# Feed-forward input products by seven quarter products: sums of weight quarters by accumulating transfers, gated tiles split at the output product

## The chip, the cores and the metric

The kernel runs on one core of one Trainium2 chip. The core has TensorE (matrix products, called PE in the profile, with its weight loads as PEld), VectorE (DVE), ScalarE (ACT), GpSimd (POOL) and SyncE (SP, which here only issues transfers). The engines run side by side and wait for one another through semaphores; transfers between the chip's memory and the core's on-chip memory run on 16 DMA engines. The metric is the device time of one execution in microseconds (us); lower is better.

## The reference

Two layers of a trunk over 512 tokens of width 1024, all in float32. Each layer is, in this order: half of a gated feed-forward, a mixer (a state-space scan and an attention side by side), half of a second gated feed-forward, and a gated per-layer input. What matters here is the feed-forward, which occurs four times:

```
def swiglu_ffn(x, w_in, w_out):
    g, u = jnp.split(x @ w_in, 2, axis=-1)
    return (jax.nn.silu(g) * u) @ w_out

h = x + 0.5 * swiglu_ffn(rms_norm(h, ffn1_norm[i]), ffn1_w_in[i], ffn1_w_out[i])
```

`w_in` is 1024 x 5632 (2816 columns for `g`, 2816 for `u`), `w_out` is 2816 x 1024. The input product `x @ w_in` is a 512 x 1024 by 1024 x 5632 product.

## The kernel before, in words

**Layout.** Activations are kept transposed: features lie in the 128 partitions, the 512 tokens along the free axis. A feature tile is 128 x 512; there are 8 of them for the trunk `h` and 22 (`KF`) for the hidden layer.

**Precision.** Each float32 operand is split into two parts of a faster type, `hi` (a rounded copy, made by ACT) and `lo` (the rest, made by DVE). A product of a weight block and a feature tile is then three matmuls: `hi` by `hi`, `hi` by `lo`, `lo` by `hi` (`acc_wx`, L344 to L346).

**Weights.** `plan_layer` lists every weight unit in the order in which the products take them. A unit is up to 128 x 1024 numbers, 512 KB. `load_one` issues its transfer on SP into one of `NRAW` = 4 buffers called `raw` (L226); `split_one` makes `hi` (L240, ACT) and `lo` (L241, DVE) in one of `NW` = 3 pairs of buffers. `weights(key)`, called before each product, keeps the transfers `LOOK_DMA` = 5 units and the splits `LOOK_SPLIT` = 2 units ahead.

**The order of the work.** The Python code fixes which instruction works on what and the order of priority. The order in which each engine executes them is made when the program is built, from a model of the execution: an instruction whose inputs and buffers are there can be put ahead of earlier ones. 74 buffers of 128 x 512 (`slots`) and 8 banks for results (`banks`) are handed out in the order in which they came free, which also limits how far ahead an instruction can go.

**The feed-forward** (`ffn`). The norm of the input (`Norm`) puts its gain into the operands as each tile of `h` is finished (`add_operand`, L382 and L383) and adds up the squares; the factor per token, `norm.rb`, is applied later. For each of the 22 tiles `f` there is one product for `g` and one for `u`, 24 matmuls of 512 columns each. `evac` then takes the pair out of its banks: DVE multiplies `g` by the factor per token (L465), ACT applies SiLU (L467), DVE multiplies by `u` (L468), and the result is split at once into `hi` and `lo` (`halves`, L357 and L358), which stay for the output product. The output product makes 8 tiles, each over all 22 hidden tiles in three weight units; DVE scales (L500), adds to `h` (L502), and the next norm's operand and square follow.

**Around it.** Before the first feed-forward, `x` comes in by 8 transfers (L274) and is transposed on TensorE (L1252). Before the second one the mixer's last output products finish tiles of `h`. After the second comes the per-layer input (`ple`), whose two loads (`ple_load`, L1146) are issued before that feed-forward. In the mixer, POOL does some products and sums (L773, L804), and attention keeps its probabilities in slots (`pr` in `scores`).

Of the kernel before, what the change touches and what calls it, by code (L numbers as in the profile page):

```python
# [17 lines left out]
P = 128  # L18
# [21 lines left out]
NSLOT = 74  # L40
NRAW = 4
NW = 3
LOOK_DMA = 5
LOOK_SPLIT = 2

# 2*pi as a sum of pieces; the first two have 12 bits, so that 11 bits times them are exact
# [20 lines left out]
class _Slots:  # L67
    """Buffers of one size, each with a tag of its own, handed out in the order they came free."""
# [17 lines left out]
def kernel(ctx: ExitStack, tc: tile.TileContext, a: dict, out: bass.AP):  # L86
# [20 lines left out]

    def sm(tag, shape, dt=F32, bufs=None):
        uid[0] += 1
        return small.tile(list(shape), dt, tag=tag, name=f"{tag}_{uid[0]}", bufs=bufs)  # L110
# [8 lines left out]
    units = []  # L119

    def unit(key, nk, cols, *loads):
        units.append((key, nk, cols, loads))
# [4 lines left out]
    def plan_ffn(i, nm, w_in, w_out):  # L127
        for f in range(KF):
            unit((i, nm, "g", f), KD, P, (None, kview(w_in, 0, KD, f * P, P)))
            unit((i, nm, "u", f), KD, P, (None, kview(w_in, 0, KD, FF + f * P, P)))  # L130
# [74 lines left out]
    loaded, split = [], []  # L205
    later = deque()

    def load_one():
        for _ in range(4 if len(loaded) > 2 else 0):
            if later:  # L210
                later.popleft()()
        key, nk, cols, loads = units[len(loaded)]
        raw = p_raw.tile([P, 1024], F32, tag="raw", name=f"raw{len(loaded)}")
        v = raw[:, :nk * cols].rearrange("p (k f) -> p k f", k=nk)
        for where, src in loads:
# [10 lines left out]
            nc.sync.dma_start(out=dst, in_=src)  # L226
        loaded.append((raw, nk, cols))
# [4 lines left out]
    def split_one():  # L232
        j = len(split)
        while len(loaded) <= j:
            load_one()
        raw, nk, cols = loaded[j]
# [3 lines left out]
        A.copy(hi[:, :n], raw[:, :n])  # L240
        V.tensor_tensor(lo[:, :n], raw[:, :n], hi[:, :n].bitcast(F32), op=ALU.subtract)  # L241
        loaded[j] = None
# [3 lines left out]
    taken = [0]  # L246

    def weights(key):
# [3 lines left out]
        while len(loaded) < min(j + 1 + LOOK_DMA, len(units)):  # L252
            load_one()
# [53 lines left out]
    tri = const.tile([P, P], F32, name="tri")        # 1 where row <= column  # L307
    stri = const.tile([P, P], F32, name="stri")      # 1 where row > column
# [6 lines left out]
    mk_l = const.tile([P, P], BF16, name="mk_l")     # row 0: queries of the first chunk  # L315
    mk_r = const.tile([P, P], BF16, name="mk_r")     # row 0: keys of the second chunk
# [44 lines left out]
    class Norm:  # L361
        """RMS norm over the feature tiles added to it: the gain goes into the products'
        operand, the per-token factor is applied to what the products give."""
# [26 lines left out]
        def add_part(self, y, src, cs):  # L390
            """Some columns of the last tile."""
# [6 lines left out]
        def add_square(self, src):  # L398
            if self.acc is None:
                self.acc = S()  # L400
                A.activation(self.acc.ap, src, AF.Square)
            else:
                sq = S()
                A.activation(sq.ap, src, AF.Square)
                V.tensor_tensor(self.acc.ap, self.acc.ap, sq.ap, op=ALU.add)
                slots.put(sq)
# [45 lines left out]

    def gain(i, nm):
        return lambda k: vcol(i, nm, k)
# [4 lines left out]
    def ffn(i, nm, norm, nxt, start=lambda: None, tables=lambda: None):  # L459
        hid = []  # L460

        def evac(bg, bu):
            # the per-token factor of `u` is applied after the output product
            g = S()
            V.tensor_tensor(g.ap, bg.ap, norm.rb.ap, op=ALU.mult)  # L465
            banks.put(bg)
            A.activation(g.ap, g.ap, AF.Silu)  # L467
            V.tensor_tensor(g.ap, bu.ap, g.ap, op=ALU.mult)  # L468
            banks.put(bu)
            hi, lo = S(F32R), S(F32R)  # L470
            halves(g.ap, hi.ap, lo.ap)
            slots.put(g)
            hid.append((hi, lo))

        X = norm.ops
        held = []
        for f in range(KF):
            bg, bu = B(), B()
            acc_wx(bg.ap, weights((i, nm, "g", f)), X)
            if f == 0:  # L480
                start()
                norm.stats()
            if f == 2:
                norm.spread()
            acc_wx(bu.ap, weights((i, nm, "u", f)), X)
            held.append((bg, bu))
            if f >= 2:
                for pair in held:
                    evac(*pair)
                held = []  # L490
            if f == 4:
                tables()
        norm.drop(rb=False)
        H = [(p.ap, q.ap) for p, q in hid]
        for m in range(KD):
            b = B()
            for k0 in range(0, KF, 8):
                acc_wx(b.ap, weights((i, nm, "o", m, k0)), H, k0, k0 == 0, k0 + 8 >= KF)
            t = S()
            V.scalar_tensor_tensor(out=t.ap, in0=b.ap, scalar=0.5, in1=norm.rb.ap, op0=ALU.mult, op1=ALU.mult)  # L500
            banks.put(b)
            V.tensor_tensor(h[m].ap, h[m].ap, t.ap, op=ALU.add)  # L502
            slots.put(t)
            nxt.add(h[m].ap)
        slots.put(norm.rb)
        for p, q in hid:
            slots.put(p, q)

# [4 lines left out]
    def rope_tables():  # L513
# [23 lines left out]
        # the turns were counted from a rounded quotient: one may be left  # L537
# [16 lines left out]
    def rotate(src, cosv, sinv, n):  # L554
        """src: [P, n, 64] rows to rotate; cosv and sinv of that shape. A buffer [P, n, 64]."""
# [10 lines left out]
    def merge(dense, sparse, every):  # L566
        """Issue `sparse`'s steps in between `dense`'s, one for each `every` us of the latter."""
# [12 lines left out]
    def mixer(i, norm, nxt):  # L580
# [11 lines left out]
        # dt and the rotary key  # L592
# [7 lines left out]
        def conv_a(j, b):  # L600
            """Evacuate tile j of xBC and convolve it."""
# [14 lines left out]
        # decays and steps, with tokens in the partitions  # L616
# [46 lines left out]
        # cumulated log decays: from the chunk's start, to its end, and the whole  # L663
# [12 lines left out]
        # rotary key, doubled for the two halves of the queries  # L676
# [215 lines left out]
        # latents of queries and keys  # L892
# [91 lines left out]
        def scores(hd, qb):  # L984
# [15 lines left out]
            pr = S()  # L1000
# [8 lines left out]
        # where the blocks of the transposed probabilities lie: buffer and first column  # L1009
# [3 lines left out]
        def flip(hd, qb, pr, pt):  # L1013
# [4 lines left out]
            slots.put(pr)  # L1018
# [294 lines left out]
```

## Time and profile before

| what | value |
|---|---|
| median of 3 runs | 2345.74 us (2345.72 to 2346.37) |
| span of the profiled execution, first to last instruction | 2343.0 us; no other time of it is given, and the runs' median is 2.7 us above it |
| TensorE busy | 2330.0 us, 99% of the span |
| VectorE, ScalarE, GpSimd busy | 1245.1, 885.3, 126.0 us |
| transfers | 209.73 MB, 90 GB/s in the mean; SP's queue takes 30.6% of the 16 engines' time |
| granted TensorE clock | 0.999 of full speed |

The profile is of one execution. "Busy" for TensorE counts from the start of a matmul to its modelled end, and since matmuls are pipelined these lengths overlap; what one costs in a stream is read from the distance between starts. Lines such as L344 are lines of the kernel before, and a line can be that of a helper which many places call. In the lists of groups a row has the line, the engine, the operation, output and input with their shapes, the count, the busy time in us and the mean length in ns, and behind the last bar the idle time before these instructions with what ended it.

### The profile page before, as it was taken

The numbers are of one execution on the slowest core, as the hardware profiler recorded it, in microseconds if no ns is written. First come the engines' busy times: TensorE is split into PE (matmuls) and PEld (weight loads), VectorE is DVE, ScalarE is ACT, GpSimd is POOL, SyncE is SP. The second block draws the span as 40 slices with busy tenths as digits, with TensorE's granted clock in tenths as the row PEclk, the third lists the DMA queues.
The fourth block names the chain that finished last, engine by engine and source line by source line (L and its number), as shares of the span: only waits on it lengthen the run. The fifth ranks groups of instructions, "written<-read, shape, count | busy, mean of one in ns | idle before, by whom it ended". The sixth has DMA issues, their size and how long they took to land.

```text
span 2343.0 us, 27624 instructions
## 1 busy us (share of the span) xinstructions
PE 2330.0 (99%) x10950; PEld 1933.4 (83%) x10950; DVE 1245.1 (53%) x1944; ACT 885.3 (38%) x1388; POOL 126.0 (5%) x136
## 2 busy tenths in 40 slices
PE   9999999999999999999999999999999999999998
PEld 7888888888888888888888888888888888888887
DVE  5543345688676434434644443466876764443345
ACT  4322224455455322222432222244544543222224
POOL 0000000223000000000000000011320000000000
PEclk9999999999999999999999999999999999999999
DMA  5333333221222333332333333332112223333322
GB/s 159 97 99 98 91 96 102 88 61 43 75 81 72 100 99 99 92 95 88 100 103 99 92 95 99 95 101 82 49 53 64 93 74 106 96 94 95 99 75 84
DMA packets 396110, 209.73 MB, mean 90 GB/s; under 512 B 19438, under 2 KB 390348, under 8 KB 395980
## 3 DMA queue, kind: packets, MB, share of 16 engines
q1 hardware_dynamic: 395980, 207.96, 30.6%
q8 instruction: 86, 1.41, 0.3%
q14 instruction: 44, 0.36, 0.0%
HBM read 205.83 MB, written 2.10 MB: 89 GB/s over the span
## 4 chain that ended last, share of the span: by engine, by line
PE 99%; DMA 0%; SPq 0%; DVE 0%; ACT 0%; POOL 0%; issue 0%
PE b L344 28%; PE b L345 28%; PE b L346 28%; PE b L353 2%; PE b L352 2%; PE b L354 2%; PE b L852 1%; PE b L1017 1%; PE b L1043 0%; PE b L833 0%; PE b L836 0%; PE b L993 0%; PE b L990 0%; PE b L1044 0%; PE b L992 0%; PE b L991 0%
## 5 line engine op out<-in xcount | busy, mean ns | idle before, releaser
L344 PE MATMUL b<-s,hi 128*128 128x512 f32 (+2 forms) x2906 | 1139.1, 393 | 0.0
L346 PE MATMUL b<-s,lo 128*128 128x512 f32 (+2 forms) x2906 | 1131.2, 390 | 0.0
L345 PE MATMUL b<-s,hi 128*128 128x512 f32 (+2 forms) x2906 | 1130.9, 390 | 0.0
L240 ACT CAST hi<-raw 128x1024 fp32r<-128x1024 f32 (+3 forms) x428 | 412.1, 963 | 1121.7 <-PE b L345 656.2
L241 DVE TENSOR_TENSOR lo<-raw,hi 128x1024 fp32r<-128x1024 f32 (+3 forms) x428 | 480.6, 1124 | 349.7 <-ACT hi L240 338.7
L346 PEld LDWEIGHTS b<-s,lo 128*128 128x128 f32 (+1 forms) x2906 | 545.4, 188 | 113.4
L344 PEld LDWEIGHTS b<-s,hi 128*128 128x128 f32 (+1 forms) x2906 | 545.8, 188 | 112.6 <-issue 2.4
L345 PEld LDWEIGHTS b<-s,hi 128*128 128x128 f32 (+1 forms) x2906 | 545.7, 188 | 112.5 <-issue 2.9
L468 DVE TENSOR_TENSOR s<-b,s 128x512 f32<-128x512 f32 x88 | 60.5, 691 | 254.6 <-PE b L346 250.9
L465 DVE TENSOR_TENSOR s<-b,s 128x512 f32<-128x512 f32 x88 | 60.1, 690 | 202.3 <-PE b L346 202.3
L430 POOL TENSOR_TENSOR nr<-nv,half 128x4 f32<-128x4 f32 (+1 forms) x14 | 19.1, 1366 | 1759.9 <-DVE nv L422 1759.1
L357 ACT CAST s<-b 128x128 fp32r<-128x128 f32 (+2 forms) x196 | 66.8, 360 | 102.6 <-DVE s L358 34.0
L358 DVE TENSOR_TENSOR s<-b,s 128x128 fp32r<-128x128 f32 (+2 forms) x196 | 75.4, 402 | 33.2 <-ACT s L357 31.7
L352 PE MATMUL b<-hi,s 128*128 128x512 f32 (+1 forms) x208 | 77.9, 375 | 0.0
L353 PE MATMUL b<-hi,s 128*128 128x512 f32 (+1 forms) x208 | 77.2, 371 | 0.0
L354 PE MATMUL b<-lo,s 128*128 128x512 f32 (+1 forms) x208 | 76.2, 366 | 0.0
L358 DVE TENSOR_TENSOR s<-s,s 128x512 fp32r<-128x512 f32 x104 | 71.0, 685 | 1.1 <-ACT s L357 0.7
L357 ACT CAST s<-s 128x512 fp32r<-128x512 f32 x104 | 64.6, 622 | 5.6 <-DVE s L976 4.6
L382 ACT ACTIVATE s<-s,vec 128x512 fp32r<-128x512 f32 x56 | 40.4, 722 | 56.4 <-DVE s L502 46.7
L608 DVE SCALAR_TENSOR_TENSOR s<-s,vec,s 128x511 f32<-128x511 f32 (+2 forms) x72 | 60.8, 848 | 0.6
L500 DVE SCALAR_TENSOR_TENSOR s<-b,s 128x512 f32<-128x512 f32 x32 | 22.1, 692 | 65.4 <-PE b L346 65.4
L467 ACT ACTIVATE s<-s 128x512 f32<-128x512 f32 x88 | 54.8, 626 | 0.4
(221 smaller groups left out, 1612.9 us busy)
## 6 DMA issues: line engine op xcount, KB each, us to landing
raw<-in_ffn_w_in_dram SPq DMA_DIRECT2D x176, 512.0 KB
raw<-in_ffn_w_out_dram SPq DMA_DIRECT2D x64, 512.0 KB
raw<-in_w_in_mix_dram SPq DMA_DIRECT2D x50, 512.0 KB
raw<-in_w_out_mix_dram SPq DMA_DIRECT2D x32, 512.0 KB
raw<-in_ffn_w_out_dram SPq DMA_DIRECT2D x32, 384.0 KB
raw<-in_w_ple_gate_dram SPq DMA_DIRECT2D x16, 512.0 KB
raw<-in_w_q_b_dram SPq DMA_DIRECT2D x16, 192.0 KB
s<-in_x_dram SPq DMA_DIRECT2D x8, 256.0 KB
```

Of the source, the lines that this page charges most:

```text
L240: A.copy(hi[:, :n], raw[:, :n])
L241: V.tensor_tensor(lo[:, :n], raw[:, :n], hi[:, :n].bitcast(F32), op=ALU.subtract)
L344: mm(b, lhsT=hi[:, kk, cs], rhs=xh, start=st, stop=False)
L345: mm(b, lhsT=hi[:, kk, cs], rhs=xl, start=False, stop=False)
L346: mm(b, lhsT=lo[:, kk, cs], rhs=xh, start=False, stop=en)
L352: mm(b, lhsT=xh[:, cs], rhs=hi[:, kk], start=first, stop=False)
L353: mm(b, lhsT=xl[:, cs], rhs=hi[:, kk], start=False, stop=False)
L354: mm(b, lhsT=xh[:, cs], rhs=lo[:, kk], start=False, stop=last)
L357: A.copy(hi, src)
L358: V.tensor_tensor(lo, src, hi.bitcast(F32), op=ALU.subtract)
L468: V.tensor_tensor(g.ap, bu.ap, g.ap, op=ALU.mult)
L608: V.scalar_tensor_tensor(out=y[:, s:], in0=x[:, :T - s], scalar=wc(3 - s), in1=y[:, s:], op0=ALU.mult, op1=ALU.add)
```

## The change

The input product is done by blocks of 2 x 2 quarters: tokens in two halves of 256 (`HT`), the 8 feature tiles in even and odd ones (paired as `e`, `o`), and weight columns in two halves of 256 within groups of 512. There are 11 groups for each feed-forward: five for `g` and five for `u` of four hidden tiles each (`GROUPS`), and a last one, `"m"`, with two tiles of `g` and two of `u`. For a group seven products of quarters (Strassen's scheme in the form with 15 additions) take the place of eight.

- **Operands.** `NormQ` takes the place of `Norm` ahead of a feed-forward. Per pair of feature tiles it makes four half-width sums or differences (three on DVE, one on POOL) and splits the seven half-width operands, which occupy 28 slots until the last group has used them.
- **Weight quarters.** Products 1, 2 and 3 take a quarter as it is loaded (by SP, 512 KB each, with rows of 256 columns). Products 5, 6, 4 and 7 take sums: 5 is the buffer of 1 with another quarter added, 6 that of 5 with one more, 4 that of 6, and 7 that of 3. The addition is a transfer issued by POOL that adds what it loads to what the buffer holds (`accum_op=ADD`), issued when the buffer's previous content has been split.
- **Order.** In step `n` the products are 1 of group n, 7 of n-1, 5 of n, 4 of n-1, 3, 6 and 2 of n (`ORDER`). A product is 24 matmuls of 256 columns, into a bank of two tiles by 256 tokens. Products are accumulated onto one another in the bank where they can be; in between, ACT copies a bank aside (`copied`) and DVE adds or subtracts (`combined`).
- **Gating.** `finish` applies the factor per token and SiLU to a `g` group and keeps the result, and multiplies it by the `u` group when that is done. The tiles stay in float32 (22 slots) and are split into `hi` and `lo` ahead of the first output tile, by halves of the tokens.
- **Buffers.** 71 slots for 74; 6 `raw` buffers for 4; transfers are kept 3 loads ahead of the split. Temporaries of the output product and of the sums of squares, and attention's probabilities, come from the `raw` buffers (`tmp`). The loads of the per-layer input go behind the last output tile (`between`).

The core of the diff:

```diff
+ORDER = ((1, 0), (7, 1), (5, 0), (4, 1), (3, 0), (6, 0), (2, 0))
+GROUPS = [(x, q) for q in range(KF // 4) for x in "gu"] + [("m", KF // 4)]
...
+            first = {1: (0, 0), 2: (1, 0), 3: (1, 1)}
+            after = {5: (1, 0, 1), 6: (5, 1, 1), 4: (6, 1, 0), 7: (3, 0, 1)}
...
+        if j in more:
+            held[more[j]] = x
+            _, nk, cols, _, (_, loads) = units[more[j]]
+            place_in(x, nk, cols, loads,
+                     lambda dst, src: G.dma_start(out=dst, in_=src, accum_op=ALU.add))
...
+        def quarters(self, e, o):
+            a11, a21, a12, a22 = e[:, :HT], e[:, HT:], o[:, :HT], o[:, HT:]
+            s, t = S(), S()
+            s1, s2, s3, s4 = s[:, :HT], s[:, HT:], t[:, :HT], t[:, HT:]
+            V.tensor_tensor(s1, a21, a22, op=ALU.subtract)
+            V.tensor_tensor(s2, s1, a11, op=ALU.subtract)
+            G.tensor_tensor(s3, a11, a21, op=ALU.subtract)
+            V.tensor_tensor(s4, a12, s2, op=ALU.add)
+            for p, x in ((1, a11), (2, a12), (5, s1), (6, s2), (4, a22), (7, s3), (3, s4)):
+                y = S(F32R)
+                halves(x, y[:, :HT], y[:, HT:])
+                self.O[p].append(y)
...
+        def product(bank, n, p, first):
+            hi, lo = weights((i, nm, n, p))
+            ops = norm.O[p]
+            for f in range(2):
+                o = bank[:, f * HT:(f + 1) * HT]
+                cs = slice(f * P, (f + 1) * P)
+                for k in range(4):
+                    x = ops[k]
+                    more = dict(skip_group_check=not first)
+                    mm(o, lhsT=hi[:, k, cs], rhs=x[:, :HT], start=first and f == k == 0, stop=False, **more)
+                    mm(o, lhsT=hi[:, k, cs], rhs=x[:, HT:], start=False, stop=False, **more)
+                    mm(o, lhsT=lo[:, k, cs], rhs=x[:, :HT], start=False, stop=f == 1 and k == 3, **more)
...
+                if m == 0:
+                    for f in range(k0, k0 + nk):
+                        hi, lo = S(F32R), S(F32R)
+                        for a in range(2):
+                            ts = slice(a * HT, (a + 1) * HT)
+                            halves(hid[a][f // 2][:, (f % 2) * HT:(f % 2 + 1) * HT], hi[:, ts], lo[:, ts])
+                            if f % 2:
+                                slots.put(hid[a][f // 2])
```

More of the change, by code (lines that the diff above doesn't have):

```diff
@@ L106, with tmp @@
     uid = [0]
+    def tmp():
+        uid[0] += 1
+        return p_raw.tile([P, 1024], F32, tag="raw", name=f"tmp{uid[0]}")[:, :T]
     def sm(tag, shape, dt=F32, bufs=None):
@@ L116, with raw @@
     G = nc.gpsimd
+    raws = []
     units = []
+    def raw(nk, cols, *loads):
+        raws.append((nk, cols, loads))
+        return len(raws) - 1
     def unit(key, nk, cols, *loads):
-        units.append((key, nk, cols, loads))
+        units.append((key, nk, cols, raw(nk, cols, *loads), None))
     def kview(w, k0, nk, c0, n):
@@ L203, with place_in @@
         plan_layer(i)
-    loaded, split = [], []
+    loaded, split, held = [], [], {}
     later = deque()
[L208 to L214, printed above, removed]
+    more = {u[4][0]: j for j, u in enumerate(units) if u[4] is not None}
+    def place_in(t, nk, cols, loads, start):
+        v = t[:, :nk * cols].rearrange("p (k f) -> p k f", k=nk)
         for where, src in loads:
@@ L225, in load_one @@
                     dst = v[:, k, h * 64:(h + 1) * 64]
-            nc.sync.dma_start(out=dst, in_=src)
-        loaded.append((raw, nk, cols))
+            start(dst, src)
+    def load_one():
+        for _ in range(4 if len(loaded) > 2 else 0):
+            if later:
+                later.popleft()()
+        t = p_raw.tile([P, 1024], F32, tag="raw", name=f"raw{len(loaded)}")
+        place_in(t, *raws[len(loaded)], lambda dst, src: nc.sync.dma_start(out=dst, in_=src))
+        loaded.append(t)
     def small_load(out, in_):
@@ L233, in split_one @@
         j = len(split)
-        while len(loaded) <= j:
-            load_one()
-        raw, nk, cols = loaded[j]
+        _, nk, cols, r, _ = units[j]
+        if r is not None:
+            while len(loaded) <= r:
+                load_one()
+            held[j] = loaded[r]
+        x = held.pop(j)
         n = nk * cols
@@ L451, with __init__, add_operand, drop_product @@
         rb = None
+    class NormQ(Norm):
+        def __init__(self, *args):
+            super().__init__(*args)
+            self.O = {p: [] for p in range(1, 8)}
+            self.pair = []
+        def add_operand(self, src, operand=True):
+            w = self.gain(self.k)
+            self.k += 1
+            x = S()
+            A.activation(x.ap, src, AF.Copy, scale=w)
+            self.pair.append(x)
+            if len(self.pair) == 2:
+                e, o = self.pair
+                self.pair = []
+                self.quarters(e, o)
+                slots.put(e, o)
+        def quarters(self, e, o):
[10 more added lines that the diff above has]
+                self.O[p].append(y)
+            slots.put(s, t)
+        def drop_product(self, p):
+            slots.put(*self.O.pop(p))
     def gain(i, nm):
```

183 lines of the change are left out of this document (124 added, 59 removed).

## The prediction

> **What bounds the kernel now.** I read the page's busy shares first, then its chain, then TensorE in order of time where its matmuls narrow, then the other engines by stretches.
>
> ```profile
> span 2343.0 us, 27624 instructions
> PE 2330.0 (99%) x10950; PEld 1933.4 (83%) x10950; DVE 1245.1 (53%) x1944; ACT 885.3 (38%) x1388; POOL 126.0 (5%) x136
> PE 99%; DMA 0%; SPq 0%; DVE 0%; ACT 0%; POOL 0%; issue 0%
> ```
>
> The chain is TensorE for 99% of the span, so a matmul saved is time saved as long as nothing else becomes late. The profile's "busy" is a pipelined length, so I price a matmul by the distance between starts. Near the end the kernel itself goes from 512 to 256 moving columns (TensorE in order of time; start, length, line):
>
> ```profile
> 2290.49 0.39 PE L344 MATMUL b<-s,hi 128*128 128x512 f32 x1
> ...
> 2323.15 0.39 PE L344 MATMUL b<-s,hi 128*128 128x512 f32 x1
> ...
> 2323.83 0.28 PE L344 MATMUL b<-s,hi 128*128 128x256 f32 x1
> ...
> 2329.22 0.28 PE L344 MATMUL b<-s,hi 128*128 128x256 f32 x1
> ```
>
> 144 matmuls lie between the first two starts: 32.66/144 = 0.2268 us. 45 lie between the last two: 5.39/45 = 0.1198 us. Half the columns cost 53% rather than 50%: 107.0 ns for 256 columns plus 12.8 ns fixed. Each matmul also has its weight load; 187 to 192 ns long, so I looked at whether loads hold up the narrow ones:
>
> ```profile
> 2324.06 0.19 PEld L344 LDWEIGHTS b<-s,hi 128*128 128x128 f32 x1
> 2324.18 0.19 PEld L345 LDWEIGHTS b<-s,hi 128*128 128x128 f32 x1
> ```
>
> They start 0.12 apart and overlap; the load does not set 0.188 as the pace.
>
> **The change, part by part.** *Matmuls.* Before, four feed-forwards make 44 tiles each from 8 weight blocks with 3 matmuls: 4 x 44 x 8 x 3 = 4224 of 512 columns, 958.0 us. After, 4 x 11 groups x 7 products x 24 = 7392 of 256 columns, 885.6 us. Saved: 72.4 us. One eighth of 958 would be 120; the fixed 12.8 ns on 3168 more instructions and their share takes the rest.
>
> The Trainium skill (TensorE: Matmul & The Clock Gate, "Back-to-back issue gap") gives N/2.4 + 2.5 ns between warm matmuls, so about 109 and 216 ns; an estimate from it would be a saving of 104 us. The trace has a fixed part of 12.8 ns, not 2.5, and decides.
>
> *Evacuations in the input stage.* Rows for the pieces (groups by line with shapes kept apart):
>
> ```profile
> L240 ACT CAST hi<-raw 128x1024 fp32r<-128x1024 f32 x342 | 359.2, 1051 | 946.9 <-PE b L345 538.5 <-issue 383.8 <-PE b L353 22.8
> L241 DVE TENSOR_TENSOR lo<-raw,hi 128x1024 fp32r<-128x1024 f32 x342 | 422.2, 1235 | 322.3 <-ACT hi L240 311.5
> L465 DVE TENSOR_TENSOR s<-b,s 128x512 f32<-128x512 f32 x88 | 60.1, 690 | 202.3 <-PE b L346 202.3
> L467 ACT ACTIVATE s<-s 128x512 f32<-128x512 f32 x88 | 54.8, 626 | 0.4
> L1245 ACT COPY s<-b 128x512 f32<-128x512 f32 x4 | 2.3, 579 | 0.0
> L358 DVE TENSOR_TENSOR s<-b,s 128x256 fp32r<-128x256 f32 x16 | 6.7, 419 | 1.6 <-ACT s L357 1.6
> L383 DVE SCALAR_TENSOR_TENSOR s<-s,vec,s 128x512 fp32r<-128x512 f32 x56 | 41.9, 749 | 24.1 <-ACT s L382 24.1
> ```
>
> A group lasts 168 x 0.1198 = 20.1 us on TensorE. DVE then has 7 weight splits (8.6), 3 combinations and 4 finishes (7 x 0.69 = 4.8): 13.4 us. ACT has 7 casts (7.4), 3 copies (1.7) and, in a gate group, 4 SiLU (2.5): 11.6 us. Both lie under TensorE; a bank's copy or combination has one product of another bank (2.87 us) as cover, where it needs under 0.7 (uncovered only in the first and last group). Cost 0.
>
> *Operands at a feed-forward's start.* Instead of one 0.749 us DVE step per tile (6.0 us for 8) there are, per pair, three half-width sums and seven half-width splits on DVE (one more sum is POOL's): 4 x 10 x 0.42 = 16.8, so 10.8 us more, and ACT gets 28 half-width casts for 8 full ones. Where that lands (busy time by stretches; columns: stretch, its length, then busy us of PE, PEld, DVE, ACT, POOL, granted clock, DMA share, GB/s):
>
> ```profile
> 6.00:21.00 15.00, 13.11 (x54) 10.65 (x53) 13.78 (x19) 12.45 (x21) 0.00 (x0) 1.00 1.01 254
> 747.00:765.00 18.00, 18.00 (x81) 14.90 (x80) 17.52 (x25) 13.10 (x20) 0.00 (x0) 1.00 0.39 114
> 1170.00:1180.00 10.00, 10.00 (x46) 8.29 (x45) 5.94 (x8) 3.78 (x5) 0.00 (x0) 1.00 0.53 157
> 255.00:275.00 20.00, 20.00 (x90) 16.57 (x89) 7.43 (x9) 5.65 (x7) 0.00 (x0) 1.00 0.32 94
> ```
>
> At the kernel's start (first row) and before a second feed-forward (second row; it comes twice) DVE is full, so the last operand comes 10.8 us later. TensorE can take the other three pairs of the first three products meanwhile, 54 x 0.1198 = 6.5 us. Exposed: 4.3 to 10.8; I take 6 three times. Before layer 1's first feed-forward (third row) DVE is 59% busy: 0 to 4, I take 2. Together 20 us (13 to 36). Next late there is nothing: the groups behind have slack.
>
> *Gated tiles split at the output product.* 44 half-width splits, 18.5 us of DVE, leave the loop and stand before the first output tile, which is 66 x 0.2268 = 15.0 us long. The fourth row shows DVE with 7.43 of 20 us already used there: if all splits ran there, 7.4 + 18.5 - 20 = 6 us would show, 24 for four. But the written order isn't the executed one; work with its inputs ready is drawn forward:
>
> ```profile
> 27.21 0.17 DVE L653 TENSOR_SCALAR d_a<-d_a 128x16 f32<-128x16 f32 x1 [6.07 <-ACT d_a L641]
> ```
>
> This line belongs to the mixer, whose stage follows the whole first feed-forward. The splits can start as buffers come free (each product of the last group frees four), so most fit into DVE's free third of the last group. I take 1 us each, 4 in all (0 to 24).
>
> *Weight traffic.* SP's 176 input loads become 132, and 176 accumulating transfers go to POOL's queue, where nothing else waits in this stage. Each waits until its buffer's previous content is split. Tightest link, quarter 1 to quarter 5: a split starts two products ahead and takes 2.3 us:
>
> ```profile
> 120.26 1.06 ACT L240 CAST hi<-raw 128x1024 fp32r<-128x1024 f32 x1 [3.84 <-PE b L345]
> 121.35 1.23 DVE L241 TENSOR_TENSOR lo<-raw,hi 128x1024 fp32r<-128x1024 f32 x1 [0.21 <-ACT hi L240]
> ```
>
> (120.26 to 122.58). Product 5 comes two products after product 1, so the transfer has 4 x 2.87 - 2 x 2.3 = 6.9 us before TensorE waits. If it is late, ACT's cast of that quarter waits, behind it on ACT the next cast and bank copies, and TensorE waits for those. No accumulating transfer stands in this trace. Nearest rows, plain loads at the start and elsewhere:
>
> ```profile
> 1.25 2.05 SPq L274 DMA_DIRECT2D s<-in_x_dram  x4
> 4.20 2.04 PE L1252 MATMUL b<-ident,s 128*128 128x128 f32 x8 [1.59 <-DMA s<-in_x_dram]
> 2.00:10.00 8.00, 4.25 (x17) 3.04 (x17) 3.88 (x8) 4.69 (x6) 0.64 (x4) 1.00 1.02 271
> 680.00:690.00 10.00, 10.00 (x54) 8.14 (x53) 6.73 (x21) 3.96 (x12) 0.00 (x0) 1.00 0.46 155
> L430 POOL TENSOR_TENSOR nr<-nv,half 128x4 f32<-128x4 f32 x12 | 17.7, 1477 | 1711.7 <-DVE nv L422 1711.0 <-DVE nv L427 0.7
> ```
>
> 256 KB land 2.9 us after issue; the other 256 KB at 271 GB/s add 1.0: 3.9 us for a plain quarter, the lower end (a plain copy's work is contained in it, so no gain below). Upper end: source, destination and sum each moved like a plain copy, 3.9 + 2 x 1.9, plus 1.5 for POOL as in its L430: 9.2. The middle is 6.6, just inside 6.9: I take 0, and up to (9.2 - 6.9) x 44 = 101 us. Volume: rows of 1 KB go at 155/0.46 = 337 GB/s of full engines, so a group's three plain loads need 4.7 us and four accumulations 6.2 at plain price, 18.7 at three times it: 10.9 to 23.4 us against 20.1, so 0 to 3.3 x 44 = 145 us.
>
> The Trainium skill speaks against cheap sums: Collectives: The Full Stack ("The bandwidth ceiling: the fold count and why AG ≠ RS ≠ AR") says an add in the transfer engines halves the rate because it reads two sources through one ring. An estimate by it is 4.7 + 12.5 = 17.2 of 20.1 us, which still fits. No run so far shows it.
>
> *Small moves.* The two loads of the per-layer input go behind the output product; the gate's first product (24 x 0.2268 = 5.4 us) covers their 2.9, else some 3 us twice. Temporaries and attention probabilities share the six load buffers: 0, at worst 10 us.
>
> **Sum.** 2343.0 - 72.4 + 20 + 4 = 2294.6 against the profiled span; the median of the runs is 2.7 us above that span, so about 2297.
>
> **Rivals.**
> 1. *Accumulations late (other side).* From 6.9 us on each group loses the excess. The gain of 48 is eaten at 48/44 = 1.1 us, at 8.0 us per transfer; at 9.2 the time is 2398, and by volume at three times the plain price 2442. For it: the bounds include it, nothing in the trace measures it, and 86% of the engines' time would go at a price of two copies. Against: the engines are at 0.32 of their time now (fourth row of the stretches), and the later links (5 to 6, 3 to 7) have 2.9 us more each.
> 2. *Everything hidden.* If TensorE finds enough ready work at the starts and before the output, 24 falls to 0: 2273. For it: TensorE is busy 18.00 of 18.00 in the second row, with DVE full there as well. Against: DVE's 10.8 us are real, and the 6.5 us of cover are less.
> 3. *Nothing drawn forward.* 36 at the starts, 24 at the outputs, 10 of buffers: 2343.0 - 72.4 + 70 + 2.7 = 2343, no change.
> 4. *The narrow pace doesn't last.* At one load per 0.188 us, 7392 would cost 1390 us: 2800. The 45 starts exclude it but for a per cent.
>
> **How the numbers follow.** Forecast 0.45 (2283 to 2325), hidden 0.16, nothing drawn forward 0.10, late accumulations 0.28, the pace 0.01. A measurement of this kernel tells 0.2% (5 us). Faster: 0.45 + 0.16 and half of rival 3: 0.66. Same: 0.05. Slower: 0.29. The range leaves out under a tenth below and some of the dearer half of rival 1: 2268 to 2425; the faster cases' own is 2268 to 2330.
>
> **What would show it.** Input matmuls of 256 columns at 0.12 us starts and about 20 us per group; TensorE idle mostly within 15 us of a feed-forward's start, released by DVE splits of operands; no idle at the output's start. Rival 1: ACT's weight casts released by DMA, once per group, and TensorE gaps at every fifth product. I am wrong if TensorE has gaps inside the groups, or if its starts in the new products lie further apart than 0.122.

## The result, and the profile after

The changed kernel takes 2496.06 us (median of 4 runs, 2493.02 to 2501.34) against 2345.73 us before: 1.0643 times as long, with a 95% interval of 1.0628 to 1.0658. The forecast was 2297, and its range ended at 2425. The profiled execution of the changed kernel took 2493.02 us, 1.8 us more than its span.

The page of the changed kernel: span, engines, the two transfer queues, the chain.

```profile
span 2491.2 us, 35639 instructions
PE 2334.5 (94%) x14118; PEld 2071.8 (83%) x14118; DVE 1512.1 (61%) x2440; ACT 1120.2 (45%) x1860; POOL 381.1 (15%) x344
...
q1 hardware_dynamic: 288972, 184.89, 25.4%
q0 software_dynamic: 101376, 92.29, 24.9%
...
PE 64%; DMA 19%; DVE 6%; issue 6%; ACT 4%; POOL 1%; SPq 1%; ACTq 0%; POOLq 0%; DVEq 0%
```

The chain that was TensorE for 99% now goes through transfers for 19% and through DVE, ACT and "issue" for another 16%. The queue rows give the price of an addition. Plain loads (q1) moved 184.89 MB in 25.4% of the engines' span, which is 292 GB/s of full engines; adding transfers (q0) moved 92.29 MB in 24.9%, which is 149 GB/s: half.

Where the time goes is read from TensorE's waits and from what ACT waits for (engine, line, what it waited for: us in all, times, longest).

```profile
PE b L567 <- ACT hi L286: 87.9, 50, 4.6
PE b L569 <- DVE lo L287: 18.0, 18, 4.5
PE b L568 <- DVE s L413: 14.9, 8, 4.0
...
PE b L401 <- DVE lo L287: 5.4, 4, 1.5
```

```profile
ACT hi L286 <- DMA raw<-in_ffn_w_in_dram: 291.9, 67, 8.2
```

L286 is ACT's cast of a weight quarter, L567 the first matmul that uses it. So the sign that the prediction gave for rival 1 is there: casts released by transfers, and TensorE released by casts. It is inside the groups, as TensorE in order of time shows for the steady part of the first feed-forward (all its waits of over half a microsecond between 60 and 215 us; start, length, line, and in brackets the idle time before):

```profile
63.21 0.39 PE L567 MATMUL b<-s,hi 128*128 128x256 f32 x1 [2.92 <-ACT hi L286]
88.61 0.58 PE L567 MATMUL b<-s,hi 128*128 128x256 f32 x1 [3.24 <-ACT hi L286]
111.55 0.39 PE L567 MATMUL b<-s,hi 128*128 128x256 f32 x1 [1.12 <-ACT hi L286]
135.17 0.39 PE L567 MATMUL b<-s,hi 128*128 128x256 f32 x1 [2.96 <-ACT hi L286]
158.31 0.39 PE L567 MATMUL b<-s,hi 128*128 128x256 f32 x1 [0.99 <-ACT hi L286]
184.01 0.58 PE L567 MATMUL b<-s,hi 128*128 128x256 f32 x1 [4.65 <-ACT hi L286]
207.33 0.39 PE L567 MATMUL b<-s,hi 128*128 128x256 f32 x1 [1.41 <-ACT hi L286]
```

One gap per group, 22.9 to 25.7 us apart, where a group was forecast at 20.1. It is always at the same place of a group. The casts of weights come in the order 1, 7, 5, 4, 3, 6, 2, and a transfer is issued after the casts of 1, 5, 3 and 6 but not after 7, 4 and 2; that pattern tells which cast is which. Around the gap at 184.01, on ACT and on POOL:

```profile
161.91 1.05 ACT L286 CAST hi<-raw 128x1024 fp32r<-128x1024 f32 x1 [1.12 <-PE b L568]
...
171.24 2.00 ACT L286 CAST hi<-raw 128x1024 fp32r<-128x1024 f32 x2 [5.16 <-DMA raw<-in_ffn_w_in_dram]
...
173.62 1.05 ACT L286 CAST hi<-raw 128x1024 fp32r<-128x1024 f32 x1
182.92 1.05 ACT L286 CAST hi<-raw 128x1024 fp32r<-128x1024 f32 x1 [8.24 <-DMA raw<-in_ffn_w_in_dram]
183.87 0.58 ACT L596 COPY s<-b 128x512 f32<-128x512 f32 x1
```

```profile
164.50 1.28 POOL L295 DMA_DIRECT2D raw<-in_ffn_w_in_dram  x1 [3.26 <-DVE lo L287]
173.84 1.28 POOL L295 DMA_DIRECT2D raw<-in_ffn_w_in_dram  x1 [8.05 <-DVE lo L287]
177.43 1.28 POOL L295 DMA_DIRECT2D raw<-in_ffn_w_in_dram  x1 [2.31 <-DVE lo L287]
```

The cast at 161.91 is product 1's. Its quarter's transfer for product 5 starts on POOL at 164.50, and the cast of 5 can go at 171.24: 6.7 us. ACT had waited 5.2 us for it; TensorE, which begins product 5 at 173.06, felt 0.3 us of that (before its matmul at 173.60, below). Then the transfer for 6 starts at 173.84, with the one for 7 beside it from 177.43, and 6's cast goes at 182.92: 9.1 us. TensorE's gap ends 1.09 us later. Every gap in the fence above follows a cast of product 6. Five of the seven casts had waited for their transfer (2.6 to 8.2 us). The two before the smallest gaps, at 111.55 and 158.31, ACT shows as released by TensorE; but they too went 5.9 us after POOL's transfer for 6 (104.52 to 110.45 and 151.36 to 157.22), which is about as long as a landing takes (6.2 us in the median, see e2).

TensorE's and VectorE's rows show one thing more:

```profile
173.60 0.39 PE L569 MATMUL b<-s,lo 128*128 128x256 f32 x1
...
185.09 0.41 PE L569 MATMUL b<-s,lo 128*128 128x256 f32 x1
...
188.60 0.40 PE L569 MATMUL b<-s,lo 128*128 128x256 f32 x2
```

```profile
175.92 1.22 DVE L287 TENSOR_TENSOR lo<-raw,hi 128x1024 fp32r<-128x1024 f32 x1
183.99 1.23 DVE L287 TENSOR_TENSOR lo<-raw,hi 128x1024 fp32r<-128x1024 f32 x1 [6.86 <-ACT hi L286]
```

TensorE's order, made when the program was built, is not quite `ORDER`: the first two matmuls of product 6 (184.01 and 184.39) stand ahead of all of product 3. The matmul at 185.09 already uses a `lo`, while VectorE ends the `lo` of 6 only at 185.22 (183.99 + 1.23), so it belongs to 3; the rest of 6 follows from 188.60, where two L569 stand side by side. The weights of product 3 were split by 177.14, but it is accumulated onto the bank of product 5, and ACT's copy of that bank stands behind the cast of 6 (183.87). So the late cast of 6 held up the 2.87 us of product 3 as well. No run changes this order alone.

A gap costs more than its idle time (stretch, length, then busy us of PE, PEld, DVE, ACT, POOL, granted clock, DMA share, GB/s):

```profile
179.00:184.00 5.00, 0.37 (x4) 0.16 (x2) 0.01 (x1) 1.08 (x2) 0.00 (x0) 0.99 1.16 192
184.00:187.50 3.50, 3.49 (x16) 3.49 (x17) 2.95 (x3) 1.39 (x2) 1.28 (x1) 0.52 0.02 3
187.50:194.00 6.50, 6.50 (x56) 6.50 (x55) 2.70 (x3) 2.58 (x3) 1.28 (x1) 1.00 0.81 169
```

While two adding transfers run, the engines are full (first row). After the gap TensorE gets half its clock for 3.4 us (second row: 0.52, and 16 matmuls where the last row's pace would make 30). The Trainium skill (TensorE: Matmul & The Clock Gate, "Part 1: The HAM clock gate") has the clock halved after an idle window of some 3.4 us, until some 3.4 us of work have passed. The trace agrees where the gap was 4.65 us and the half clock 3.4; after the shorter gap of 2.92 us at 63.21 the clock was 0.50 from 64.5 to 67.9 as well.

### The profile page after: what moved, and what is told of

Its sections match the earlier page's. It is cut to its first block, busy times and chain, and to the rows that moved or that the text cites. A ratio compares the mean times of both kernels' runs of the same rounds, so it can differ in the third digit from the quotient of the medians.

```text
span 2491.2 us, 35639 instructions
## 1 busy us (share of the span) xinstructions
PE 2334.5 (94%) x14118; PEld 2071.8 (83%) x14118; DVE 1512.1 (61%) x2440; ACT 1120.2 (45%) x1860; POOL 381.1 (15%) x344
## 3 DMA queue, kind: packets, MB, share of 16 engines
q1 hardware_dynamic: 288972, 184.89, 25.4%
q0 software_dynamic: 101376, 92.29, 24.9%
## 4 chain that ended last, share of the span: by engine, by line
PE 64%; DMA 19%; DVE 6%; issue 6%; ACT 4%; POOL 1%; SPq 1%; ACTq 0%; POOLq 0%; DVEq 0%
DMA raw<-in_ffn_w_in_dram 19%; PE b L399 13%; PE b L401 13%; PE b L400 13%; PE b L567 5%; PE b L568 4%; PE b L569 4%; ACT hi L286 3%; DVE lo L287 3%; PE b L407 1%; PE b L408 1%; PE b L409 1%; PE b L1017 1%; DVE s L413 1%; PE b L1182 1%
## 5 line engine op out<-in xcount | busy, mean ns | idle before, releaser
L287 DVE TENSOR_TENSOR lo<-raw,hi 128x1024 fp32r<-128x1024 f32 (+3 forms) x560 | 642.1, 1149 | 685.5 <-ACT hi L286 684.4
L286 ACT CAST hi<-raw 128x1024 fp32r<-128x1024 f32 (+3 forms) x560 | 547.7, 981 | 968.9 <-PE b L400 372.9
L567 PE MATMUL b<-s,hi 128*128 128x256 f32 x2464 | 726.0, 295 | 102.3 <-ACT hi L286 87.9
L568 PE MATMUL b<-s,hi 128*128 128x256 f32 x2464 | 715.8, 291 | 14.9 <-DVE s L413 14.9
L569 PE MATMUL b<-s,lo 128*128 128x256 f32 x2464 | 709.5, 291 | 18.1 <-DVE lo L287 18.0
L567 PEld LDWEIGHTS b<-s,hi 128*128 128x128 f32 x2464 | 489.6, 199 | 123.4 <-ACT hi L286 100.1
L399 PE MATMUL b<-s,hi 128*128 128x512 f32 (+1 forms) x1498 | 590.6, 396 | 0.0
L401 PE MATMUL b<-s,lo 128*128 128x512 f32 (+1 forms) x1498 | 584.0, 391 | 5.4 <-DVE lo L287 5.4
L400 PE MATMUL b<-s,hi 128*128 128x512 f32 (+1 forms) x1498 | 582.2, 389 | 0.0
L569 PEld LDWEIGHTS b<-s,lo 128*128 128x128 f32 x2464 | 486.4, 199 | 22.9 <-DVE lo L287 22.6
L568 PEld LDWEIGHTS b<-s,hi 128*128 128x128 f32 x2464 | 489.9, 199 | 17.8 <-DVE s L413 17.5
L295 POOL DMA_DIRECT2D raw<-in_ffn_w_in_dram x192 | 247.6, 1335 | 803.4 <-DVE lo L287 757.5
L401 PEld LDWEIGHTS b<-s,lo 128*128 128x128 f32 x1498 | 280.7, 187 | 66.2 <-DVE lo L287 7.7
L400 PEld LDWEIGHTS b<-s,hi 128*128 128x128 f32 x1498 | 281.1, 188 | 58.1 <-issue 2.9
L399 PEld LDWEIGHTS b<-s,hi 128*128 128x128 f32 x1498 | 281.2, 188 | 56.7 <-issue 2.4
L413 DVE TENSOR_TENSOR s<-s,s 128x256 fp32r<-128x256 f32 (+1 forms) x304 | 118.9, 433 | 4.3 <-ACT s L412 3.9
L596 ACT COPY s<-b 128x512 f32<-128x512 f32 x132 | 76.5, 579 | 8.7 <-PE b L569 8.7
```

Of the source, the lines that this page charges most:

```text
L286: A.copy(hi[:, :n], x[:, :n])
L287: V.tensor_tensor(lo[:, :n], x[:, :n], hi[:, :n].bitcast(F32), op=ALU.subtract)
L295: lambda dst, src: G.dma_start(out=dst, in_=src, accum_op=ALU.add))
L399: mm(b, lhsT=hi[:, kk, cs], rhs=xh, start=st, stop=False)
L400: mm(b, lhsT=hi[:, kk, cs], rhs=xl, start=False, stop=False)
L401: mm(b, lhsT=lo[:, kk, cs], rhs=xh, start=False, stop=en)
```

## The experiments

Two theories stood at first: that the adding transfers are late (their price), and that something which comes with them is (issue by POOL, the waits, 69 MB more). Later two readings of the price had to be told apart: full engines, or single landings on links that are too short. All kernels are variants of the changed one; "link" is the number of products, in the order of `ORDER`, from the use of a quarter to the use of the sum made in its buffer. In the changed kernel the links are 1→5: 2, 5→6: 3, 3→7: 4, 6→4: 5.

**e1_no_sum: no adding transfers.** Products 5, 6, 4 and 7 then use quarters without the sum.

```diff
-            place_in(x, nk, cols, loads,
-                     lambda dst, src: G.dma_start(out=dst, in_=src, accum_op=ALU.add))
```

> The 176 pairs of accumulating transfers (192 issues) are left out: products 5, 6, 4 and 7 split and use the buffer as it was, so these products are computed from unsummed quarters; everything else is that of the changed kernel. Theory A (the accumulating transfers land after ACT's casts need them, and that alone turned the gain into a loss): about 2300 us, the forecast for everything else, with groups of 20.1 us and granted clock back at 1.00. Rival B (the narrow products, the operands at a feed-forward's start or DVE's extra work cost it): 2440 us or more. If half comes back, about 2400, both have a part.

Measured: 2328.31 us (one run; before 2347.95 on the same chip), 28 above theory A's 2300 and far below rival B. Its busy times, its span with the granted clock, and those of the changed kernel:

```profile
PE 2278.2 (98%) x14118; PEld 2039.5 (88%) x14118; DVE 1521.1 (65%) x2440; ACT 1132.9 (49%) x1860; POOL 136.5 (6%) x152
```

```profile
core 0: 2326.5 us, clock 0.989
```

```profile
core 0: 2491.2 us, clock 0.978
```

Both TensorE's idle time (span less busy: 48.3 us, 156.7 with the transfers) and what the mean granted clock takes from the span (1.1% and 2.2% of it, 25.6 and 54.8 us) come down.

**e2_plain_pool: the same transfers without the addition.**

```diff
-                     lambda dst, src: G.dma_start(out=dst, in_=src, accum_op=ALU.add))
+                     lambda dst, src: G.dma_start(out=dst, in_=src))
```

> The same transfers in the same places of POOL's queue with the same waits, but they overwrite the buffer instead of adding to it, so products 5, 6, 4 and 7 use unsummed quarters. Theory A1 (adding makes the transfer about twice as dear per byte, 149 GB/s of full engines against some 300, and this is what makes it late): landing falls from 6.2 us to 4.5 or less, time within 20 us of the kernel without the transfers, about 2300 to 2320. Rival A2 (the link itself, issue by POOL and the wait for the split, costs it whatever the transfer does): landing stays near 6, time above 2430.

Measured: 2327.69 us, span 2326.0, within 20 us of e1 as theory A1 asked, though 8 above its 2320. The list of issues of the changed kernel (output and input, queue, count, KB, median us to landing), then the same list and the queue row of this one:

```profile
raw<-in_ffn_w_in_dram POOLq DMA_DIRECT2D x160, 512.0 KB, 6.2
```

```profile
q0 software_dynamic: 25600, 92.29, 12.7%
...
raw<-in_ffn_w_in_dram POOLq DMA_DIRECT2D x160, 512.0 KB, 4.0
```

As many transfers by the same queue with the same waits and bytes cost nothing; the addition costs all of 168 us (2496 to 2328). It lands in 6.2 us where a plain transfer lands in 4.0, and takes 24.9% of the engines' time where that takes 12.7%. The packets differ too: 101376 with the addition, 25600 without. Whether the second read or the smaller packets double the price was not separated.

**e4_sum_pool and e5_sum_dve: all quarters loaded plainly by SP, the sums made by an engine.** `SUM` is GpSimd in e4, VectorE in e5; buffers for seven loads instead of six.

```diff
-                units.append((key, 4, 256, None, (at[n, before], quarter(n, kh, c))))
+                units.append((key, 4, 256, raw(4, 256, *quarter(n, kh, c)), at[n, before]))
...
+        if -j in held:
+            SUM(j).tensor_tensor(x[:, :n], x[:, :n], held.pop(-j)[:, :n], op=ALU.add)
```

> All seven quarters of a group are loaded plainly by SP, 69 slots and 7 load buffers in place of 71 and 6, and POOL adds the held quarter to the new one (176 tensor sums of 128x1024). Computes the same. If only the accumulating transfers are at fault and POOL's sum takes about 2.9 us (twice its 1.44 us for 128x512): POOL is busy 11.5 us of a 20.1 us group, time about 2300 to 2330. Rival (POOL and DVE hold each other up where both read two on-chip operands, or seven loads a group don't come in time): 2400 or more, with casts or splits of weights late behind POOL.

> As the kernel with sums on POOL, but on DVE (176 sums of about 1.23 us): DVE has 13.4 + 4.9 = 18.3 us of work in a group of 20.1. If DVE's order leaves few gaps: 2310 to 2350. Rival (DVE becomes the bound in places, its sums wait for loads and hold up evacuations): 2380 or more, TensorE released by DVE.

Measured: 2424.36 us on GpSimd, as the rival there had it, and 2361.51 on VectorE, between the two ranges expected. Groups by line with shapes kept apart, first of e4, then of e5:

```profile
L289 DVE TENSOR_TENSOR lo<-raw,hi 128x1024 fp32r<-128x1024 f32 x474 | 768.2, 1629 | 293.8 <-ACT hi L288 292.4
L285 POOL TENSOR_TENSOR raw<-raw,raw 128x1024 f32<-128x1024 f32 x176 | 504.8, 2878 | 560.8 <-DMA raw<-in_ffn_w_in_dram 286.1 <-DVE lo L289 95.9 <-DVE s L1251 63.4
```

```profile
L289 DVE TENSOR_TENSOR lo<-raw,hi 128x1024 fp32r<-128x1024 f32 x474 | 578.9, 1227 | 239.6 <-ACT hi L288 238.4
L285 DVE TENSOR_TENSOR raw<-raw,raw 128x1024 f32<-128x1024 f32 x176 | 215.4, 1224 | 117.1 <-DMA raw<-in_ffn_w_in_dram 115.4
```

A sum takes GpSimd 2.88 us and VectorE 1.22. With the sums on GpSimd, VectorE's own splits of the same shape rise from 1227 to 1629 ns: the engine that was to be relieved loses 189 us (768.2 − 578.9), nearly the 215 us that the sums would cost it. GpSimd's own 2.88 us are twice the 1.44 us of its 128x512 sum in the changed kernel, so no row shows that it was slowed. The Trainium skill (Trainium Architecture — The Big Picture, "What this means for kernel authors") says that these two engines share a port pair as an exclusive lock; the rows agree that VectorE is held up (1629 ns against 1227), but show lengths only, not the lock. On VectorE the four sums cost 33 us over e1.

**e8_one_operand: e1, and one operand per pair of tiles, `a11`, for all seven products.** What this leaves out beside the weight sums is the operand sums and six of seven operand splits.

```diff
...
-            for p, x in ((1, a11), (2, a12), (5, s1), (6, s2), (4, a22), (7, s3), (3, s4)):
-                y = S(F32R)
-                halves(x, y[:, :HT], y[:, HT:])
+            y = S(F32R)
+            halves(a11, y[:, :HT], y[:, HT:])
+            for p in self.O:
                 self.O[p].append(y)
...
```

> From the kernel without sums by transfers (2328 us): of the seven half-width operands only the first is made (its two halves of a split per pair) and all seven products read it; the four sums and six splits per pair are left out. Theory C (what is left of the forecast's miss, 2328 against about 2300, comes from the operands at the feed-forwards' starts: TensorE stalls there, and after a stall runs at half clock for 3.4 to 13.7 us): no half clock within the span's middle, 2270 to 2290 us. Rival D (it comes from inside the groups, copies and combinations or the narrow pace): 2315 or more.

Measured: 2295.43 us, somewhat above what was expected. First TensorE's longest wait at the start in e1, with stretches at the starts of three feed-forwards (columns as above); then stretches and the clock of e8. By the third of these starts e8 is ahead of e1, so its stretch there begins at 1860; its last row lies behind that start:

```profile
28.99 0.58 PE L566 MATMUL b<-s,hi 128*128 128x256 f32 x1 [4.54 <-DVE s L411]
```

```profile
14.00:31.00 17.00, 7.17 (x30) 6.18 (x29) 13.47 (x34) 11.76 (x31) 1.75 (x2) 0.67 0.30 87
...
740.00:800.00 60.00, 50.85 (x325) 46.31 (x324) 44.62 (x77) 38.19 (x69) 4.91 (x5) 0.89 0.18 53
1900.00:1960.00 60.00, 50.83 (x388) 49.22 (x387) 45.48 (x76) 37.02 (x63) 2.89 (x3) 0.89 0.27 80
```

```profile
740.00:800.00 60.00, 57.99 (x431) 55.90 (x430) 42.02 (x55) 38.24 (x57) 1.98 (x1) 0.94 0.26 80
1860.00:1920.00 60.00, 57.92 (x395) 54.28 (x394) 37.16 (x48) 35.51 (x53) 1.97 (x1) 0.94 0.23 71
...
1900.00:1960.00 60.00, 60.00 (x502) 60.00 (x502) 40.59 (x50) 33.77 (x48) 0.00 (x0) 1.00 0.26 79
```

```profile
core 0: 2293.6 us, clock 0.995
```

The operands cost 33 us in all (2328 − 2295, one run each). At the second and third of these starts TensorE is idle 9.2 us each in e1 and 2.0 and 2.1 in e8, and the granted clock is 0.89 against 0.94: shorter stalls, though not none. The mean granted clock, 0.989 and 0.995, is 25.6 and 11.5 us of full clock over the spans, 14 apart; but the clock is also low while TensorE stands idle (in e1's first stretch it is busy for 7.17 of 17 us), so not all of the 14 is time lost by slow matmuls, and how the 33 divide was not separated. The last stretch also checks the pace: 60.00/502 = 0.1195 us per narrow matmul.

**e9_order: the changed kernel with product 2 in third place.** The same transfers; the links become 1→5: 3, 5→6: 3, 3→7: 3, 6→4: 5. (The calls of the products and the first group's norm factor move with it.)

```diff
-ORDER = ((1, 0), (7, 1), (5, 0), (4, 1), (3, 0), (6, 0), (2, 0))
+ORDER = ((1, 0), (7, 1), (2, 0), (5, 0), (4, 1), (3, 0), (6, 0))
```

> The changed kernel with product 2 moved from the last to the third place of a step (its factor per token is made right behind the first product). Every link between a split and the product that needs the sum is then three products or more (1 to 5: 3 in place of 2), with the same transfers. Theory L (single landings of 6 to 9 us are too long for the shortest link): 2496 falls below 2440. Theory V (the adding transfers fill the transfer engines: 4 x 0.52 MB at 149 GB/s and 3 x 0.52 MB at 292 are 19.5 us of a 20.1 us group, so any bunching makes some link late): 2470 or more, DMA share again near 0.77.

Measured: 2385.56 us; 110 us came back with every transfer still there (92.29 and 184.89 MB, as before). A stretch within the first feed-forward, first of the changed kernel, then of this one, and this one's waits of casts for transfers:

```profile
60.00:250.00 190.00, 169.59 (x1327) 165.88 (x1326) 106.75 (x138) 79.72 (x105) 39.82 (x31) 0.96 0.78 153
```

```profile
60.00:250.00 190.00, 186.81 (x1538) 184.79 (x1537) 122.17 (x148) 99.13 (x139) 48.92 (x38) 1.00 0.90 172
```

```profile
ACT hi L286 <- DMA raw<-in_ffn_w_in_dram: 307.9, 112, 5.8
```

The mean load of the transfer engines was not the cause, then: with theirs at 0.90 instead of 0.78 TensorE is busy for 186.81 of 190 us. The casts wait more often (112 times, 67 before) but less long (5.8 us at most, 8.2 before), and TensorE's wait for casts falls from 87.9 to 32.6 us. What fits this is the chain of two links, 1→5→6, which has 6 products here and 5 in the changed kernel: the last link, 5→6, is 3 long in both, and the gaps before product 6 are mostly gone.

**e6_hybrid: products 5 and 6 summed on VectorE from plain loads, 4 and 7 by adding transfers.** The changed kernel's order, so the adding links that remain are the long ones (4 and 5 products).

```diff
+BY_DVE = (5, 6)
...
+                if p in BY_DVE:
+                    units.append((key, 4, 256, raw(4, 256, *quarter(n, kh, c)), at[n, before]))
+                else:
+                    units.append((key, 4, 256, None, (at[n, before], quarter(n, kh, c))))
```

> Sums for products 5 and 6 on DVE from plain loads, those for 4 and 7 (the longest links, five and four products) by accumulating transfers as in the changed kernel; 69 slots, 7 load buffers. Computes the same. Engines need 5 x 1.8 + 2 x 3.5 = 16.0 us of a group, DVE 13.4 + 2.5 = 15.9. Theory V: both fit, 2335 to 2350 us (half of the 33 us that four sums on DVE added to 2328). Theory L: also fits, these links allow 9.8 us and more. Rival: any accumulating transfer is late behind plain loads, 2380 or more.

Measured: 2347.74 us (10 runs), 1.0005 of before [0.9996, 1.0014]: no difference from before. Both theories had this range, so it does not tell them apart. Its waits of casts for transfers:

```profile
ACT hi L293 <- DMA raw<-in_ffn_w_in_dram: 10.1, 9, 2.4
```

The adding transfers on links of 4 and 5 products, 96 of them, cost next to nothing: 148 us of the 168 are gone, and of the 20 that remain two sums on VectorE account for 16 by estimate (half of e5's 33). There are also only half as many adding transfers here.

**e7_hybrid_pool: e6, with the three operand sums of each pair on GpSimd as well.**

```diff
-            V.tensor_tensor(s1, a21, a22, op=ALU.subtract)
+            G.tensor_tensor(s1, a21, a22, op=ALU.subtract)
```

(and likewise for `s2` and `s4`, which goes ahead of `s3`)

> As the kernel with mixed sums, and the three operand sums that DVE makes per pair go to POOL (0.96 us each there against 0.42). DVE is relieved by 5 us at each start. Theory C: stalls and half clock at the starts shrink, 10 to 25 us less than the mixed kernel. Rival: POOL's chain of three sums makes the operands as late as before, within 5 us of it or worse.

Measured: 2357.1 us, 1.0044 [1.0027, 1.0061]. TensorE's wait for operands' splits rises from 27.9 us in e6 to 36.4. The splits wait for sums that are chained (`s2` from `s1`, `s4` from `s2`), and on GpSimd the chain is later.

**e10_both: e6 with the order of e9.** The adding links that remain are 3→7 with 3 products and 6→4 with 5.

> As e6 (products 5 and 6 summed by VectorE from plain loads, 4 and 7 by adding transfers), with the order of e9 (product 2 in third place). The two adding links that are left are 5 and 3 products long instead of 5 and 4. If e6 lost nothing more to its adding transfers, 2343 to 2352, as e6 within its error. If the order itself is worth something beyond those links (product 2's bank freed earlier), 2335 to 2343.

Measured: 2379.08 us, 1.0147 [1.0126, 1.0167]. Both branches of the expectation missed: the order that brought 110 us back now costs 31. The waits of casts, then ACT and POOL around one of them:

```profile
ACT hi L293 <- DMA raw<-in_ffn_w_in_dram: 105.4, 44, 5.9
```

```profile
153.80 1.05 ACT L293 CAST hi<-raw 128x1024 fp32r<-128x1024 f32 x1 [1.59 <-PE b L576]
...
165.29 2.02 ACT L293 CAST hi<-raw 128x1024 fp32r<-128x1024 f32 x2 [4.11 <-DMA raw<-in_ffn_w_in_dram]
```

```profile
159.27 1.28 POOL L303 DMA_DIRECT2D raw<-in_ffn_w_in_dram  x1 [15.41 <-DVE lo L294]
```

44 waits, where e6 had 9. The casts shown are of 3 and 7: the transfer for 7 starts 5.5 us after the cast of 3, because VectorE has sums and combinations ahead of that split, and takes 6.0 us more. Its link went from 4 products to 3 with the order. But TensorE hardly waits for these casts (3.1 us in all). Its largest wait is for VectorE's split of weights, 2.8 us in 4 waits in e6 and here

```profile
PE b L577 <- DVE lo L294: 19.9, 24, 2.5
```

One of these 24 ends at 163.44, where the split of product 6 was done at 163.39; VectorE had made a sum first, from 161.03, after waiting 1.45 us for that sum's plain load. So the short link of 7 and VectorE's order both stand in these rows; which of them makes the 31 us was not separated, and no kernel lengthened that link alone.

**e10_late, e13_first, e14_all: VectorE's work at the starts.** e10_late is e10_both with the first two groups of a feed-forward summed by transfers; e13_first also splits the two plain quarters of a pair ahead of its sums; e14_all splits those of all four pairs ahead of any sum.

```diff
-                if p in BY_DVE:
+                if p in BY_DVE and n >= 2:
```

> As e10_both, but in the first two groups of each feed-forward products 5 and 6 are summed by transfers too; VectorE sums from the third group on. In e6 two sums of 1.2 us stand among VectorE's operand splits at 15.29 and 19.58 us. If VectorE at the starts is what e6 loses, 3 to 4 us of sums leave each of three starts, and a shorter stall also takes half clock away: 2331 to 2341. If the adding transfers are as late there as in the changed kernel, the first groups stall again: 2350 to 2365.

> As e10_late, but of each pair of operand tiles the two plain quarters (operands of products 1 and 2, which come first now) are split before the sums are made. If VectorE's order at a start sets the stall, the first two products find their operands some 1 us earlier per pair: 4 to 12 us less than e10_late. If the pairs' arrival or the total of VectorE's work sets it, the same as e10_late within 3 us.

> As e13_first, but the two plain quarters of all four pairs are split before any sum of any pair. The last operand of products 1 and 2 then stands behind 8 half-width splits, not behind 40 half-width steps; the others come no earlier. TensorE gets 48 products' matmuls (5.7 us) early at three starts: 5 to 20 us less than e10_late, by the stall and by half clock that it brings. If the whole of VectorE's work is the bound, the stall moves behind product 2 and the time stays within 4 us of e10_late.

Measured: 2383.66 (1.0157 [1.0142, 1.0172]), 2383.98 (1.0162 [1.0145, 1.0179]) and 2379.19 us (1.0136 [1.0121, 1.0152]), beside 2379.08 for e10_both. None of it gained: e10_late is above both of its ranges, as e10_both, on which all three build, already was. Neither the two early sums nor the order of operand splits sets the time at the starts of this kernel; e14_all's 4 to 5 us below e10_late and e13_first is at the edge of "within 4 us". Nothing tried that computes the same is faster than the kernel before. The nearest is e6, and e1 shows that weight sums at no cost would bring it only 20 us below before (2328.31 against 2347.95).

## Why the prediction was wrong, point by point

*The bound.* "A matmul saved is time saved as long as nothing else becomes late" held; the condition did not.

*Matmuls, 72.4 us saved.* The price was right. The pace within a product is 0.12 (0.1195 in e8), so rival 4 is out.

*Evacuations, 0.* In the changed kernel TensorE waits 5.7 us for bank copies (L596) and 4.6 for combinations (L601) in all; in e1 its waits have no such row. By themselves they cost nothing, then, but a copy behind a late cast does.

*Gated tiles, 4 us.* About right: TensorE's waits in the wide matmuls (line L401) are for VectorE's split of weights, which stands among those of the gated tiles; they come once per feed-forward, 5.4 us in all, 1.7 in e1.

*Operands at the starts, 20 us (13 to 36).* Too small. e1, with nothing of the weight sums left, has a span of 2326.5 where my sum says 2294.6: 32 us more. The step that failed is "Exposed: 4.3 to 10.8; I take 6 three times". TensorE is idle 9.8, 9.2 and 9.2 us in e1's three stretches (17.00 less 7.17, 60.00 less 50.85 and 50.83): 28 where 18 were taken, each within the 10.8. And the slow clock that comes with a stall (0.67 in the first stretch) stood in no term. Of the 32 us, e8 leaves a part unplaced: it has most of these operands left out and is still at 2293.6, where my sum without their 20 us is 2274.6. Its clock explains up to 9 us of that (0.995 against 0.999 before), the rest I did not trace.

*Weight traffic, 0.* This is the step that decided, and it cost 165 us (span 2491.2 against 2326.5 in e1). My price per transfer was fair: the middle of 6.6 against a median of 6.2, the upper end of 9.2 against 9.1 with two in flight. The link that I called the tightest, 1→5 with 6.9 us, held: 6.7 us, and 0.3 us of waiting on TensorE. What failed is the sentence "the later links (5 to 6, 3 to 7) have 2.9 us more each". (For 3 to 7, four products, it is 5.7 us more; that is not the point.) It takes each link as if its own start were on time. But 6 is made in the buffer of 5, and the cast of 5, which my price puts two products ahead of its use (173.06 − 5.74 = 167.32), went at 171.24, 3.9 us late. TensorE felt 0.3 us of that, the transfer for 6 all of it. Counted as one chain, by my own formula, 1→5→6 has 7 x 2.87 − 3 x 2.3 = 13.2 us for two transfers; two at 6.2 fit, 6.7 + 9.1 = 15.8 are 2.6 us too long. The gap at 184.01 is larger, 4.65, since TensorE takes the first matmuls of 6 two products behind 5 and not three. Counted so, the chain has 6 x 2.87 − 3 x 2.3 = 10.3 us: 15.8 are 5.5 too long, less the 1.2 us by which a cast is done before its whole split, and two at 6.2 don't quite fit either, which agrees with the gaps of about 1 us where the transfer for 6 took 5.9. In e9 one product more makes it 13.2, into which two at 6.2 fit. I read these counts from the rows; that a chain one product longer takes most of the gaps away is shown by e9. A longer look-ahead of the splits, which would lengthen every link, was not tried.

*The bounds.* 101 us by lateness and 145 by volume were both too low for 165. The granted clock is the part that neither held: 0.978 against 0.989 in e1 is 54.8 against 25.6 us, so some 29 us by the mean clock. TensorE's idle time by the page is 156.7 against 48.3 us, 108 more. These make 137 of 165; the rest is not placed by these rows, since busy lengths overlap and reach into the gaps. The bound by volume was the wrong mechanism: e9 moves the same bytes 110 us faster.

*The rule on additions.* The Trainium skill's rule that I weighed (Collectives: The Full Stack, "The bandwidth ceiling: the fold count and why AG ≠ RS ≠ AR"), which the page states for the addition of a ReduceScatter, halves the rate. The trace agrees, 149 against 292 GB/s, and the volume would still fit, with 19.5 of a group's 20.1 us (four of 0.52 MB at 149, three at 292). It was no help for the landing of a single transfer.

*Rival 1.* The right one, at 0.28, with casts released by transfers as its sign. "Every fifth product" was the wrong place: every seventh, always product 6. *Rival 2* is out: the operands were not hidden. *Rival 3*'s 36 us for the starts was near the 33 that e1 and e8 show, by the number alone, since it has no slow clock in it; its 24 for the outputs was not.

*Small moves.* No wait in the rows above points to them; not tested.

## What to carry to other kernels

When a buffer is filled, used, added to and used again, add up the slack over the whole chain of links and count the lateness of one as a debt of the next; a link that is late without being felt is not free. Take the slack from the order in which the engines execute, which need not be the written one. Price an addition by transfer at twice a plain one for the engines and at its landing with neighbours in flight, and put it where four or more products lie between: in e6, with half as many of them, it cost next to nothing there, and taking the links of two and three away brought 148 us back. A stall that comes back each group should be priced with the slow clock that follows it.

## What the runs showed of the hardware

- An adding transfer of 512 KB landed in 6.2 us in the median where a plain one by the same queue took 4.0, and its sum could be cast 9.1 us after the issue when a second one was issued 3.6 us behind it. All 192 went as 101376 packets where the plain ones were 25600.
- After 4.65 us without work TensorE ran at half clock for 3.4 us, and after 2.92 us too; at the start of e1's first feed-forward the clock was 0.67 over 17 us.
- VectorE's split of 128 x 1024 took 1629 ns in the mean in the kernel where GpSimd made sums of 2.88 us, and 1227 ns where VectorE made them itself.
